# Norm rows loaded as broadcasts, and the order of work around the last two expert units, in a decoder layer on one core

## The chip, the cores and the metric

The kernel runs on one core of a Trainium2 chip. The core has five engines with an instruction queue each: TensorE (PE; its weight loads are listed as PEld) for matrix products and transposes, VectorE (DVE), ScalarE (ACT), GpSimd (POOL), and SyncE (SP), which here does nothing but ask for transfers. The engines meet only at semaphores. The metric is the device time of one execution in microseconds (us).

## The reference

One post-norm decoder layer is computed in float32 for one sequence of 512 tokens of width 1024. Two attention branches are mixed, projected and normalised; the part that matters here is the second half:

```python
x = layer_norm(DEEPNORM_ALPHA * x + gate1 * attn_out, ln1_g[l], ln1_b[l])
u2 = x * (1.0 + scale2) + shift2
moe = hierarchical_moe(u2.reshape(B * S, D), ...)   # (1)
x = layer_norm(DEEPNORM_ALPHA * x + gate2 * moe, ln2_g[l], ln2_b[l])

# (1) for every group of experts; combine is zero except for a token's two experts
h = silu(einsum('nd,edf->nef', t, w_g[sl])) * einsum('nd,edf->nef', t, w_u[sl])
h = h * combine[:, sl, None]
out = out + einsum('nef,efd->nd', h, w_d[sl])
```

There are 32 experts of width 256 in 4 groups. A token goes to the best group, and there to the best two of 8 experts.

## The kernel before

The first 430 us are projections, attention and the first norm. The normalised rows are written to DRAM twice: `xnd` holds them for the rows 0 to 255 already scaled by ln1's gain and shift and by the factor alpha, `xhd` without. Then come the experts.

**Units.** Tokens are sorted by expert into slots. Two experts (a pair, 64 rows each) or four (a quad, 32 rows each) make one unit with a row tile of 128. There are 12 units; the last two, unit 10 and unit 11, are quads. A unit is worked through in these steps: gate and up products (`gate_up`, L1352, 64 matmuls into one bank `pgu`), Silu on ScalarE and the product with up on VectorE (`act_h`, L1360 and L1361), the transpose of the result (`h_tr`, L1367, and `h_copy`, L1375), down products (`down`, L1382, two halves of 16 matmuls for a quad), evacuation times `gate2` (`y_evac`, L1392), and a scatter of the rows to the DRAM tensor `Ys` (`y_store`, L1398, on GpSimd). Larger tiles of a unit (`tiles`) are behind branches on the counted rows; here they aren't taken.

**Weights.** They rotate through 15 buffers (`ex_3506` and the like). `load_gran` (L940 for gate and up, L943 for down) is called for the second unit after the present one, right behind the present one's evacuation, and asks on SyncE. A request for an expert with no tokens moves nothing. SyncE's requests take eight semaphores in turn, so each waits until the transfer eight places before it is done.

**Order.** The engines TensorE, GpSimd and SyncE take their instructions in the order in which the code is written (`manual_schedule`). VectorE and ScalarE are ordered by a scheduler, except in the first and the last part, which is written out too.

**The last unit's result** isn't scattered. It stays on the chip, and its rows are added by a product with a selection matrix: `select_rows` (L1433 to L1437, GpSimd) builds for each of four token tiles which of the unit's rows belongs to which token, with which weight; `select_tr` (L1447 and L1448) turns this by eight transposes on TensorE and two copies on ScalarE. `diagonals` makes eight diagonal matrices of the tokens' weights on VectorE.

**Norm rows.** The gains and shifts of both norms have 1024 numbers each, and are wanted on all 128 partitions. `norm_rows` loads all four into 16 rows of a small tile early among the units, `scale_rows` multiplies ln1's by alpha with three small VectorE operations, and `broadcast` (L1460, L1461) spreads one row by products of a column of the identity with the small tile, which ScalarE copies out. ln2's two are spread behind `select_tr`, ahead of unit 10's down products; ln1's two between the two halves of the last unit's gate and up products. At an earlier place, in the middle of the kernel, ln1's two rows are loaded as broadcasts straight from DRAM instead, and scaled on ScalarE (L964 and L965); that place is the same in both kernels.

**Branch.** Ahead of the last unit stands `overflow()` (L1465 and L1466), a branch for experts with more tokens than their slot, which isn't taken here. All five engines pass it. Behind it SyncE asks for the rows of `xnd` and `xhd` (L1619, L1620).

**Tail.** For each of four row tiles of 128 tokens, TensorE adds up in two banks of 512 columns: the last unit's selected rows (`add_sel`, L1672), for the right half the residual (`add_x`, L1669) and the two rows gathered from `Ys` times the diagonals (`add_dg`, L1679). For the left half VectorE adds the residual (`base`, L1683) and the gathered rows (`add_y`, L1686). The moments, the norm and the output follow (L1690 to L1746). The gathered rows are asked for by SyncE at L1660, two requests of 0.52 MB for each row tile. GpSimd scales the residual of row tiles 2 and 3 with ln1's rows (`scaled`, L1646 and L1649).

## Time and profile before

| what | value |
| --- | --- |
| median of the runs shown | 787.19 us (786.98 to 790.57, 3 runs) |
| the profiled execution, its own time | 786.38 us |
| its span from the first to the last instruction | 784.70 us |
| mean granted clock of TensorE | 0.937 of full speed |
| busy: TensorE | 678.0 us, 86% of the span |
| busy: VectorE, ScalarE, GpSimd | 480.5, 252.5, 173.8 us |
| transfers | 184.13 MB, 235 GB/s in the mean |

The rows further down come from one profiled execution. Times are counted from the span's start. The execution's own time is 1.68 us longer than the span. The busy shares are means over stages with different limits. In timelines, neighbouring instructions of one form stand in one row with their count; in brackets is the engine's idle time ahead of the row and what the trace takes to have ended it. "PEq" or "POOLq" as releaser is the queue of an engine at a branch.

### The profile page before, as it was taken

To read this page: it belongs to the slowest core of one execution; us is meant where nothing else is said; L and a number is where in the kernel's file an instruction comes from. 1 tells how busy PE (TensorE), PEld (TensorE's weight loads), DVE (VectorE), ACT (ScalarE), POOL (GpSimd) and SP (SyncE) were. 2 spreads that over 40 slices of the span, in tenths; PEclk is the share of its full clock that TensorE was granted. 3 is DMA by queue.
4 is the path that set the end of the run, shared out by engine and by line. 5 is a ranking of instruction groups with operands and counts; after the bars stand their busy time and mean duration, and the time that the engine had idled before them with its cause. 6 is when DMAs were issued, how large, how long until landed. Compare 5 with 4: busy or idle time off the path is not lost. (4 is left out here: it accounts for less than half of the span.)

```text
span 784.7 us, 10759 instructions
## 1 busy us (share of the span) xinstructions
PE 678.0 (86%) x3361; PEld 426.8 (54%) x3361; DVE 480.5 (61%) x1070; ACT 252.5 (32%) x546; POOL 173.8 (22%) x240
## 2 busy tenths in 40 slices
PE   5999998989989998799999873977699699976983
PEld 4778766556757765566788662432363223333321
DVE  3353479877775558977595686774825606551158
ACT  2233344433333434444341453622101101122221
POOL 2007024122233313200000013111111101155155
PEclk9999999999999999999999895889899989996897
DMA  9959763365653011361369468796999989799652
GB/s 281 360 159 332 241 200 107 112 220 200 221 168 107 18 31 42 108 196 54 107 215 368 169 259 295 236 389 241 411 407 417 386 342 351 280 404 395 236 215 107
DMA packets 83230, 184.13 MB, mean 235 GB/s; under 512 B 15201, under 2 KB 48590, under 8 KB 77274
## 3 DMA queue, kind: packets, MB, share of 16 engines
q1 hardware_dynamic: 76608, 171.71, 60.9%
q0 software_dynamic: 6480, 11.53, 4.2%
q8 instruction: 37, 0.61, 0.3%
q14 instruction: 31, 0.25, 0.1%
q10 hardware_dynamic: 74, 0.03, 0.0%
HBM read 173.28 MB, written 28.33 MB: 257 GB/s over the span
## 5 line engine op out<-in xcount | busy, mean ns | idle before, releaser
L1352 PE MATMUL pgu<-ex,xT 128*64 128x512 f32 (+1 forms) x608 | 116.1, 619 | 9.9 <-DMA ex<-in_w_exp_up_dram 5.8
L330 PE MATMUL acc<-uh,whi 128*128 128x512 f32 x224 | 91.8, 410 | 1.1 <-ACT whi L320 1.1
L330 PE MATMUL acc<-uh,wlo 128*128 128x512 f32 x224 | 89.1, 398 | 2.4 <-DVE wlo L321 2.4
L1352 PEld LDWEIGHTS pgu<-ex,xT 128*64 128x64 f32 (+1 forms) x608 | 52.4, 130 | 69.4 <-issue 63.8
L330 PE MATMUL acc<-ul,whi 128*128 128x512 f32 x224 | 89.1, 398 | 0.0
L1382 PE MATMUL py<-ex,hT 128*64 128x512 f32 (+1 forms) x304 | 63.8, 673 | 10.8 <-DVE rtx L1392 4.4
L628 POOL TENSOR_TENSOR w<-be,sc 128x128 f32<-128x128 f32 (+3 forms) x32 | 41.8, 1314 | 119.8 <-DVE sc L626 60.6
L1360 ACT ACTIVATE sl<-pgu 128x256 f32<-128x256 f32 x33 | 11.5, 382 | 167.7 <-PE pgu L1352 122.9
L321 DVE TENSOR_TENSOR wlo<-raw,whi 128x1024 fp32r<-128x1024 f32 x27 | 38.9, 1448 | 21.4 <-ACT whi L320 17.8
L330 PEld LDWEIGHTS acc<-uh,wlo 128*128 128x128 f32 x224 | 42.6, 190 | 14.8 <-DVE wlo L321 3.5
L1398 POOL DMA_INDIRECT Ys<-w,msk_mla x11 | 10.9, 989 | 178.2 <-DVE w L1392 150.2
L330 PEld LDWEIGHTS acc<-uh,whi 128*128 128x128 f32 x224 | 42.8, 191 | 11.7 <-ACT whi L320 1.6
L330 PEld LDWEIGHTS acc<-ul,whi 128*128 128x128 f32 x224 | 42.9, 192 | 9.0 <-issue 0.8
L1361 DVE TENSOR_TENSOR sl<-pgu,sl 128x256 f32<-128x256 f32 x33 | 12.9, 418 | 52.0 <-ACT sl L1360 47.8
L1382 PEld LDWEIGHTS py<-ex,hT 128*64 128x64 f32 (+1 forms) x304 | 16.8, 134 | 51.1 <-issue 30.5
L449 DVE SCALAR_TENSOR_TENSOR macc<-ra,rtx,macc 128x1024 f32<-128x1024 f32 x28 | 41.5, 1523 | 3.6 <-DMA ra<-in_w_ada_dram 3.6
L626 DVE TENSOR_TENSOR_SCAN sc<-al 128x127 f32<-128x127 f32 (+3 forms) x32 | 28.7, 921 | 12.7 <-ACT al L622 12.7
L320 ACT CAST whi<-raw 128x1024 fp32r<-128x1024 f32 x27 | 28.1, 1050 | 24.9 <-PE acc L330 9.8
L1375 DVE COPY hT<-phT 128x256 f32<-128x256 f32 x33 | 13.1, 418 | 37.3 <-PEq L1408 21.8
L563 PE MATMUL px<-ident,w 128*128 128x128 f32 x160 | 26.7, 279 | 9.2 <-POOL w L628 5.0
L563 PEld LDWEIGHTS px<-ident,w 128*128 128x128 f32 x160 | 18.5, 142 | 17.5 <-issue 7.1
L895 PE MATMUL oh<-wo,mixh 128*128 128x512 f32 x64 | 23.9, 430 | 1.4 <-DVE wo L877 1.4
(494 smaller groups left out, 1387.1 us busy)
## 6 DMA issues: line engine op xcount, KB each, us to landing
ex<-in_w_exp_gate_dram SPq DMA_DIRECT2D x64, 512.0 KB
ex<-in_w_exp_up_dram SPq DMA_DIRECT2D x64, 512.0 KB
ex<-in_w_exp_down_dram SPq DMA_DIRECT2D x32, 1024.0 KB
ra<-in_w_ada_dram SPq DMA_DIRECT2D x16, 1024.0 KB
raw<-in_w_in_dram SPq DMA_DIRECT2D x12, 1024.0 KB
ada<-in_w_ada_dram SPq DMA_DIRECT2D x6, 1024.0 KB
rwo<-in_w_out_dram SPq DMA_DIRECT2D x6, 1024.0 KB
Ys<-dqh SPq DMA_DIRECT2D x8, 512.0 KB
```

The costliest lines, as they stand in the source:

```text
L320: ACT.copy(hi, w)
L321: DVE.tensor_tensor(lo, w, hi.bitcast(F32), ALU.subtract)
L330: PE.matmul(a, w_[:, k, :], part(u_, k), start=(k == 0 and n == 0), stop=(k == nk - 1 and n == 2))
L449: DVE.scalar_tensor_tensor(o, v, cact[:, k, 0:1], o, ALU.mult, ALU.add)
L563: PE.transpose(px[:, kt * P:(kt + 1) * P], w[:, kt * P:(kt + 1) * P], ident)
L626: DVE.tensor_tensor_scan(sc[:, 0:W - 1][:, ::-1], al[:, 1:W][:, ::-1], al[:, 1:W][:, ::-1], 1.0, ALU.mult, ALU.bypass)
L628: POOL.tensor_tensor(w[:, 0:W], be[:, 0:W], sc[:, 0:W], ALU.mult)
L895: PE.matmul(a, u_, w_[:, k % 4, :], start=first and n == 0, stop=last and n == 2)
L1352: PE.matmul(ps_t[rows, :], xT[u, t][:, k, rows], ew[e, k // 4][:, :, k % 4, :], start=(k == 0), stop=(k == KD - 1))
L1361: DVE.tensor_tensor(sl, ps_t[:, DE:2 * DE], sl, ALU.mult)
L1375: DVE.tensor_copy(hT[u, min(t, 1)][:, t // 2], phT[:, o:o + 256].rearrange("p (k n) -> p k n", k=2))
L1382: PE.matmul(pys[nh][rows, :], hT[u, min(t, 1)][:, t // 2, k, rows], ew[e, 2][:, k, nh * 512:(nh + 1) * 512], start=(k == 0), stop=(k == 1))
```

## The change

- The four broadcasts by products, the small tile, and the loads and operations that fill it go. In their place SyncE asks for four loads behind the branch, right after those of `xnd` and `xhd`, that write each of the four rows to all 128 partitions from DRAM. ln1's two are multiplied by alpha by one ScalarE operation ahead of GpSimd's scaling of row tile 2.
- `select_rows` is called before the work of units 8 and 9, not at its end.
- `select_tr` and `diagonals` stand behind the branch, ahead of the last unit's gate and up products, which run without a break between the halves.
- A Silu of a tile of one number stands behind the branch (`warm`), and the one of the square root takes another input.
- The products of the residual for row tiles 0 and 1 (`add_x`) are written first, to follow the last unit's transposes; the banks of the sums are dealt out differently, and the tail's loop has `add_x` only for row tiles 2 and 3.

```diff
--- before.py
+++ after.py
@@ -1364,7 +1364,8 @@
         o = 256 if t == 1 else 0
         h = hs[u, min(t, 1)][:, t // 2, :].rearrange("p (q k) -> p k q", k=2)
         for k in range(2):
-            PE.transpose(phT[:, o + k * P:o + (k + 1) * P], h[:, k, :], ident)
+            i = PE.transpose(phT[:, o + k * P:o + (k + 1) * P], h[:, k, :], ident)
+        return i.ins
 
     def h_copy(u, t):
         if t >= u.ntl:
@@ -1411,19 +1412,6 @@
 
     lng1, xv, *axr = (egran[i].rearrange("p (a d) -> p a d", a=2) for i in (6, 8, 7, 9))
     lng2 = [rtx[:, 0:D], None]
-
-    lr16 = rtx[0:16, 1024:1280]
-    acol = cp.tile([16, 1], F32, name="acol")
-
-    def norm_rows():
-        for i, v in enumerate((ln2_g, ln2_b, ln1_g, ln1_b)):
-            SP.dma_start(lr16[4 * i:4 * i + 4], v[0].rearrange("(c n) -> c n", c=4))
-
-    def scale_rows():
-        DVE.reduce_sum(acol, ident[0:16, 8:16], axis=AX.X)
-        DVE.tensor_scalar(acol, acol, ALPHA - 1.0, 1.0, ALU.mult, ALU.add)
-        DVE.tensor_scalar(lr16, lr16, acol, None, ALU.mult)
-
 
     selw = gate1.rearrange("p (a t n) -> p a t n", a=2, t=NT)
 
@@ -1451,14 +1439,6 @@
         for t in range(NT):
             for j in range(2):
                 DVE.tensor_scalar(dg[:, t, j, :], ident, w12[j][:, t:t + 1], None, ALU.mult)
-
-    def broadcast(v, dst):
-        for h in range(2):
-            pb = pt("z", 2, "pb")
-            for q in range(2):
-                r = 4 * v + 2 * h + q
-                PE.matmul(pb[:, q * 256:(q + 1) * 256], ident[0:16, r:r + 1].to_broadcast([16, P]), lr16, start=True, stop=True)
-            ACT.copy(dst[:, h * 512:(h + 1) * 512], pb)
 
 
     def overflow():
@@ -1561,6 +1541,8 @@
         for n, u in enumerate(units):
             more = n + 1 < len(units)
             un = units[n + 1] if more else None
+            if 2 + NOV // 2 <= n < 4 + NOV // 2:
+                select_rows(n - 2 - NOV // 2)
             pipe = n > 0 and more and u.nb == 2 and un.nb == 2
             if pipe:
                 ps0 = pt("fil", 2, "pgu0")
@@ -1576,18 +1558,12 @@
                 last = tc.manual_schedule(engines={mybir.EngineType.DVE, mybir.EngineType.Activation})
                 last.__enter__()
             if n > 0 and not pipe:
-                h_tr(u, 0)
+                htr_at = h_tr(u, 0)
                 h_copy(u, 0)
             xcopy(n + 2, 0)
             if n > 0:
                 xcopy(n + 1, 1)
                 xcopy(n + 1, 2)
-            if n == len(units) - 2:
-                select_tr()
-                lng2[1] = tmp("whi", [D], F32, "lng2")
-                broadcast(0, lng2[0])
-                broadcast(1, lng2[1])
-                diagonals()
             py0 = [pt("z", 2, f"py0_{n}") for n in range(2)]
             down(u, 0, py0, (0,))
             tiles(u, f, lambda t: h_tr(u, t))
@@ -1616,15 +1592,18 @@
                 order.close()
                 overflow()
                 order.enter_context(tc.manual_schedule(engines=MS))
+                ACT.activation(warm, warm, AF.Silu)
+                lng2[1] = tmp("whi", [D], F32, "lng2")
                 SP.dma_start(axr[0], xnd.rearrange("(t p) d -> p t d", p=P))
                 SP.dma_start(xv, xhd[256:512, :].rearrange("(t p) d -> p t d", p=P))
+                for v, o in ((ln1_g, lng1[:, 0]), (ln1_b, lng1[:, 1]), (ln2_g, lng2[0]), (ln2_b, lng2[1])):
+                    SP.dma_start(o, v[0].partition_broadcast(P))
             if more and not pipe:
                 ps0 = pt("fil", 2, "pgu0")
-                gate_up(un, 0, ps0, range(4))
                 if n == len(units) - 2:
-                    for v in range(2):
-                        broadcast(2 + v, lng1[:, v])
-                gate_up(un, 0, ps0, range(4, KD))
+                    select_tr()
+                    diagonals()
+                gate_up(un, 0, ps0)
                 act_h(un, 0, ps0)
                 if n == 0:
                     more_tiles(1)
@@ -1632,17 +1611,14 @@
                     y_store(u, (0, 1, 2))
             if n == 2 + NOV // 2:
                 DVE.tensor_copy(ovi, ov[0:1, :, 0:2])
-            if n == 1:
-                norm_rows()
-                scale_rows()
-            if 2 + NOV // 2 <= n < 4 + NOV // 2:
-                select_rows(n - 2 - NOV // 2)
 
 
         hc = [slice(h * 512, (h + 1) * 512) for h in range(2)]
         rs = [axr[t // 2][:, t % 2, :] for t in range(NT)]
 
         def scaled(e, t):
+            if t == 2:
+                ACT.activation(lng1, lng1, AF.Copy, scale=ALPHA)
             e.tensor_tensor(rs[t].rearrange("p (q k) -> p q k", k=KD), xv[:, t % 2, :].rearrange("p (k q) -> p q k", k=KD),
                             lng1[:, 0].rearrange("p (q k) -> p q k", k=KD), ALU.mult)
             for h in (1, 0):
@@ -1659,9 +1635,9 @@
             for j in range(2):
                 SP.dma_start(gt[:, j, :], Ys[j * S + t * P:j * S + (t + 1) * P, :])
             gts.append(gt)
-        ACT.activation(warm, dg[0:1, 0, 0, 0:1], AF.Sqrt, scale=0.0)
-        sums = {(t, h): pt(b, n, "sums") for h, bs in ((0, (("fil", 2), ("fil", 2), ("m", 1), ("t", 2))),
-                                                       (1, (("av", 1), ("z", 2), ("z", 2), ("t", 2)))) for t, (b, n) in enumerate(bs)}
+        ACT.activation(warm, yb[0][0:1, 0:1], AF.Sqrt, scale=0.0)
+        sums = {(t, h): pt(b, n, "sums") for h, bs in ((1, (("fil", 2), ("fil", 2), ("z", 2), ("t", 2))),
+                                                       (0, (("av", 1), ("z", 2), ("m", 1), ("t", 2)))) for t, (b, n) in enumerate(bs)}
         for t in (2, 3):
             scaled(POOL, t)
 
@@ -1706,10 +1682,12 @@
             o = rs[t][:, hc[h]]
             e.tensor_tensor(o, o, lng2[1][:, hc[h]], ALU.add)
 
-        add_x(0)
+        for t in range(2):
+            with tc.issue_after(htr_at):
+                add_x(t)
         for t in range(NT):
             add_sel(t, 0)
-            if t:
+            if t > 1:
                 add_x(t)
             add_sel(t, 1)
             add_sel1(t)
```

TensorE, around unit 10's down products, before: `phT` are the transposes of `h`, `pse` those of the selection rows, `pb` the broadcasts, and `py_0_7389` is the left half of the down products, with the four weights' buffers behind the arrow.

```order
L1408 UNCONDITIONAL_BRANCH x2
L1367 MATMUL phT<-ident,sl 128x128 x2
L1447 MATMUL pse<-ident,gate 128x128 x8
L1460 MATMUL pb<-rtx,ident 128x256 x8
L1382 MATMUL py_0_7389<-ex_3400,hT 32x512
L1382 MATMUL py_0_7389<-ex_3506,hT 32x512
L1382 MATMUL py_0_7389<-ex_3509,hT 32x512
L1382 MATMUL py_0_7389<-ex_3658,hT 32x512
```

In the changed kernel the same eight transposes stand behind the overflow branch, ahead of the last unit's gate and up products (`pgu_7520`):

```order
L1447 COMPARE_AND_BRANCH
L1447 UNCONDITIONAL_BRANCH
L1446 UNCONDITIONAL_BRANCH x2
L1435 MATMUL pse<-ident,gate 128x128 x8
L1352 MATMUL pgu_7520<-ex_3813,xT_7018 32x512
L1352 MATMUL pgu_7520<-ex_3853,xT_7018 32x512
L1352 MATMUL pgu_7520<-ex_3855,xT_7018 32x512
L1352 MATMUL pgu_7520<-ex_3857,xT_7018 32x512
```

So the down products follow the transposes of `h` at once, and the transposes and the broadcasts that stood between have moved behind the branch, or are gone.

ScalarE, from the branch to the tail's first square root, before: `pb` are the broadcasts of ln1's rows, `sl` the last unit's Silu, `mv` the moments.

```order
L1466 UNCONDITIONAL_BRANCH x2
L1461 ACT_TABLE_LOAD
L1461 COPY ex_3506<-pb 128x512 x4
L1360 ACT_TABLE_LOAD
L1360 ACTIVATE sl<-pgu_7560 128x256
L1408 UNCONDITIONAL_BRANCH
L1360 ACTIVATE sl<-pgu_4090 128x256
L1408 UNCONDITIONAL_BRANCH x4
L1692 ACT_TABLE_LOAD
L1692 ACTIVATE mv<-mv,epsr 128x1
```

The same place in the changed kernel, where `sely` is the turned selection matrix and `ex_3506` the buffer of ln1's rows:

```order
L1446 UNCONDITIONAL_BRANCH x2
L1436 COPY sely<-pse 128x512 x2
L1360 ACTIVATE sl<-pgu_7520 128x256
L1409 UNCONDITIONAL_BRANCH
L1360 ACTIVATE sl<-pgu_4089 128x256
L1409 UNCONDITIONAL_BRANCH
L1638 ACT_TABLE_LOAD
L1638 ACTIVATE warm<-w 1x1
L1409 UNCONDITIONAL_BRANCH
L1621 ACTIVATE ex_3506<-ex_3506 128x2048
```

No table load stands ahead of the Silu there, and the one for the square root stands right behind it.

SyncE, behind the branch, before: `gt_7711` and so on are the buffers of the gathered rows.

```order
L1619 DMA ex_3509<-xnd 128x2x1024
L1620 DMA ex_3658<-xhd 128x2x1024
L1408 UNCONDITIONAL_BRANCH
L1660 DMA gt_7711<-Ys 128x1024 x2
L1660 DMA gt_7714<-Ys 128x1024 x2
```

And in the changed kernel:

```order
L1597 DMA ex_3509<-xnd 128x2x1024
L1598 DMA ex_3658<-xhd 128x2x1024
L1600 DMA ex_3506<-in_ln_g_dram 128x1024
L1600 DMA ex_3506<-in_ln_b_dram 128x1024
L1600 DMA rtx<-in_ln_g_dram 128x1024
L1409 UNCONDITIONAL_BRANCH
L1600 DMA lng_7513<-in_ln_b_dram 128x1024
L1636 DMA gt_7676<-Ys 128x1024
```

The four broadcast loads stand between the loads of rows and the requests for the gathered rows.

## Rows read from the trace of the kernel before

**Rows 1.** Chain that ended last, first and last step: start us, us, engine, output, line

```profile
765.17 0.69 DVE sums L1683
...
780.50 0.75 DVE ex L1745
```

**Rows 2.** Timeline of VectorE: start us, us, instruction, count [idle before, releaser]

```profile
732.88 0.68 DVE L1392 TENSOR_TENSOR sc<-py,gate 128x512 f32<-128x512 f32 x1
...
765.17 0.69 DVE L1683 TENSOR_TENSOR sums<-ex,sums 128x512 f32<-128x512 f32 x1 [1.07 <-PEq L1408]
```

**Rows 3.** Timeline of TensorE from 711 to 760, columns as in rows 2

```profile
711.26 0.71 PE L1447 MATMUL pse<-ident,gate 128*128 128x128 f32 x5
...
718.43 7.19 PE L1460 MATMUL pb<-rtx,ident 16*128 16x256 f32 x16
725.55 3.64 PE L1382 MATMUL py<-ex,hT 128*32 128x512 f32 x16
729.37 2.15 PE L1382 MATMUL py<-ex,hT 128*32 128x512 f32 x16 [0.18 <-PEq L1408]
732.78 4.05 PE L1352 MATMUL pgu<-ex,xT 128*32 128x512 f32 x32 [1.26 <-DMA ex<-in_w_exp_down_dram]
736.76 4.09 PE L1460 MATMUL pb<-rtx,ident 16*128 16x256 f32 x16
740.78 4.98 PE L1352 MATMUL pgu<-ex,xT 128*32 128x512 f32 x32
748.07 0.50 PE L1367 MATMUL phT<-ident,sl 128*128 128x128 f32 x2 [2.31 <-DVE sl L1361]
...
749.46 1.92 PE L1382 MATMUL py<-ex,hT 128*32 128x512 f32 x16
...
755.76 1.96 PE L1679 MATMUL sums<-gt,gate 128*128 128x512 f32 x4
...
758.41 1.02 PE L1669 MATMUL sums<-ex,ident 128*128 128x512 f32 x2
```

**Rows 4.** Timeline of GpSimd: scatter, first and last selection operation, first scaling

```profile
693.48 0.97 POOL L1398 DMA_INDIRECT Ys<-w,msk_mla  x1 [10.77 <-DVE w L1392]
...
697.09 0.55 POOL L1433 TENSOR_SCALAR onesf<-iot 128x128 f32<-128x128 f32 x1
...
717.51 0.45 POOL L1437 TENSOR_TENSOR gate<-gate,rk 128x128 f32<-128x128 f32 x1
...
746.04 2.86 POOL L1646 TENSOR_TENSOR ex<-ex,ex 128x1024 f32<-128x1024 f32 x1 [10.47 <-PEq L1408]
```

**Rows 5.** Busy us of each engine (instructions), granted clock, DMA share and GB/s by stretch

```profile
431.00:432.00 1.00, 1.00 (x6) 0.84 (x5) 1.00 (x2) 0.00 (x0) 0.00 (x0) 1.00 1.08 266
718.00:726.00 8.00, 7.98 (x21) 5.54 (x25) 0.29 (x1) 4.07 (x7) 0.00 (x0) 0.50 0.99 369
731.00:732.00 1.00, 0.52 (x8) 0.00 (x0) 0.32 (x1) 0.00 (x0) 0.00 (x0) 1.00 0.68 279
735.00:736.00 1.00, 1.00 (x15) 0.74 (x9) 0.00 (x0) 0.00 (x0) 0.57 (x1) 1.00 0.53 160
736.00:738.00 2.00, 2.00 (x13) 1.08 (x7) 0.00 (x0) 0.07 (x1) 0.00 (x0) 1.00 1.03 408
```

**Rows 6.** Timeline of SyncE's queue, last requests; columns as in rows 2

```profile
717.36 0.07 SPq L940 DMA_DIRECT2D ex<-in_w_exp_up_dram  x1
...
724.94 6.82 SPq L943 DMA_DIRECT2D ex<-in_w_exp_down_dram  x4
733.68 0.40 SPq L1619 DMA_DIRECT2D ex<-xnd  x1
...
745.92 4.60 SPq L1660 DMA_DIRECT2D gt<-Ys  x8
```

**Rows 7.** Timeline of ScalarE, at the middle and in the last part

```profile
433.77 1.91 ACT L965 ACTIVATE lng<-lng 128x2048 f32<-128x2048 f32 x1 [6.22 <-DMA lng<-in_ln_b_dram]
...
745.88 1.28 ACT L1360 ACT_TABLE_LOAD   x1 [4.41 <-PE pgu L1352]
```

## The prediction

> **What bounds the kernel now.** I read the chain that ended last first. It names VectorE alone, from 765 us to the end at 781.25, and shares out 2% of the span: it breaks off at the first wait that it can't follow [rows 1]. So the question is what released VectorE there. VectorE's timeline answers: its add for row tile 2 at 765.17 had sat idle for 1.07 us until TensorE's branch had passed [rows 2]. TensorE's timeline therefore comes next, and it has to be read backwards from there [rows 3]. In the tail it adds up the four row tiles without a pause, 4.7 us each: the gathered rows' products of the first begin at 755.76 and those of the third release VectorE at 765.17. They follow the down products of the last unit (749.46), which follow its gate and up products, which end at 745.76. Before these stand the down products of unit 10 (725.55), and before them 16 records of broadcast products that begin at 718.43, and transposes that began at 711.26. The transposes need GpSimd's selection rows, of which the last is written at 717.51 [rows 4]. That stretch is what the change takes apart. A further 16 broadcast records stand inside the last unit's gate and up products, at 736.76.
>
> The second thing to see is the transfers. The weights stream at some 400 GB/s until 731.7: in the microsecond from 731 there are 279 GB/s, 0.68 of the 408 of a full one [rows 5]. SyncE asks for the next transfer only at 733.68, and for the gathered rows at 745.92 [rows 6]. So TensorE's path can be shortened only until the stream is the limit, and what the change adds to the stream counts.
>
> The profiled execution took 786.38 us, 1.68 more than its span of 784.70; the median of the runs shown is 787.19, 0.81 above it. I sum against the profiled execution and add 0.81 at the end. Times below that stand for the changed kernel are on the old trace's scale.
>
> **The change part by part.** *Selection rows earlier.* On GpSimd the first selection moves ahead of unit 8's scatters, the second ahead of unit 9's. Both took 20.9 us from 697.09 to the end at 717.96 with two scatters of some 1.3 us each between them, so 9.1 us each [rows 4]. GpSimd had sat idle for 10.77 us ahead of unit 8's scatters at 693.48 [rows 4], which hides the first. If VectorE's overflow items hold it back, it is the scatters that come late, by up to 9.1 us. That would cost unit 10's activation at most some 2 us, and behind that the weights wait anyway (next part). I take nothing, and 2 us as the other end, also covered.
>
> *Transposes and broadcasts out of the way of unit 10's down products.* What stood ahead of them from 711.26 to 725.55 is gone: 14.3 us. But they can't start at 711.9. A SyncE request waits for the transfer eight places before it; the one at 717.36 moves nothing itself (0.07 us, its expert has no tokens) and waited for the fourth of unit 10's down loads [rows 6]. The fourth product in TensorE's order needs that load. So the start is 717.4, and I let them take what they took: 3.64 + 0.18 + 2.15, to 723.3 [rows 3]. At the rate of the last unit's (1.92 each) it would be 721.4; I take the slow one because TensorE will have idled from 712.
>
> *The transposes' new place.* They now wait for VectorE to pass the overflow branch. Its last evacuation ended at 733.56, 2.04 after the last down product [rows 2, 3]; TensorE needed 1.26 from its last product to its first behind the branch, and I give VectorE the same. So 723.3 + 2.04 + 1.26 = 726.6. Five of the transposes took 0.71 us at full rate [rows 3], so eight take 1.1, or 2.3 at half rate: 728.3 in the middle. On ScalarE the two copies that follow are beside TensorE's work, as are VectorE's eight diagonals.
>
> *Gate and up of the last unit without the broadcasts between.* The halves took 3.98 (732.78 to 736.76) and 4.98, the second after a slow start; 4.09 of broadcasts between them go [rows 3]. With 4.05 for each and half a microsecond for the slow start they end at 736.9. Their weights are there: the last to land are the two down loads of 2.1 MB, 5.1 us of stream before 731.7.
>
> *The table request.* In the order on ScalarE it brings no load with it, and the load ahead of the Silu at 745.88, 1.28 us, is gone [rows 7]. From the last product to the transposes of h there were 2.31 us; 1.03 are left: 737.9.
>
> *Four broadcast loads, 0.52 MB each, and the scaling.* Removed for them: four requests and three small VectorE operations in the middle of the kernel, where neither engine is waited for. SyncE asks for them right behind the two loads of rows, ahead of the gathered rows. All weights must have landed first (731.7); the request that used to wait for unit 10's last product, and left at 731.76 (the four from 724.94 took 6.82) [rows 6], is no longer late. I put the first request at 733.0, between 732.3 and the old 733.7. Data began 1.9 us after it (the microsecond from 735 had 160 GB/s), so at 734.9. The first row load, 1.05 MB at 408 GB/s, is there at 737.5, just ahead of the transposes that its product follows. Then: second row load and four broadcasts to 734.9 + 4.19/0.408 = 745.2, and the first pair of gathered rows to 747.8. With 0.5 us (an estimate, 0 to 1) until the waiting engine moves: 748.3.
>
> TensorE meanwhile: last down products at 737.9 + 1.39 = 739.3 instead of 749.46, the gathered rows' products 6.30 later as before (749.46 to 755.76) plus 0.9 for the second residual product, which now stands ahead: 746.5. So the gathered rows end last, at 748.3; the second half of the 1.96 us block follows: 749.3 instead of 757.72, 8.4 us earlier. The second tile then lacks its residual product (1.02 us with its drain, 0.9 without [rows 3]), so from the second tile's end on all is 9.3 us earlier, VectorE's add of 765.17 too.
>
> The scaling took 1.91 us at its other place, waiting for its own two broadcast loads [rows 7]. Here they land at 743.1 (3.15 MB and 0.5 us), behind the warm-up that waits for the last unit's first evacuation (741.9 or so): done at 745.0. GpSimd's two tiles need 2.86 and as much again each [rows 4], so they are ready at 750.7 and 756.4; they are wanted at 755.9 and 760.6. That leaves over 4 us.
>
> **Sum:** 786.38 - 9.3 + 0.81 = 777.9; I say 778.
>
> What is unknown is the rate of the broadcast loads. At the other place the microsecond that I can give to them had 266 GB/s, the lowest of that stretch [rows 5]: 7.9 us instead of 5.1, and 780.7. At no cost of their own at all TensorE's path would be last, at 746.5, and the time 777.2. I take 408, since the row loads ran at it.
>
> The Trainium skill speaks against such loads: "DMA: Bandwidth & Descriptors", section "Bandwidth", asks for at least 1 MiB per transfer to get 75% of the peak and gives 341 GB/s at 1 MB. By 341 for all six loads the pair would come 2.0 us later and the time would be 779.9; the 408 GB/s of row loads of 1.05 MB that ran two at a time [rows 5] speak for the higher rate.
>
> **Rivals.** *The last unit still waits for the stream.* The trace ends TensorE's wait at 732.78 with a down load [rows 3]. If that holds, gate and up start there and end at 740.8, the gathered products come at 750.4 and end at 752.4: 5.3 + 0.9 us gained, 781.0. Against it: in the order those products wait for gate and up loads only, and 1.26 us is what the branch may take. 12 in 100.
>
> *TensorE at half clock after each wait.* From 718 to 726 it was granted 0.50, the 1.2 GHz level, though busy, after it had stood waiting for GpSimd; 16 records of down products took 3.64 us then, and 1.92 at the other level [rows 3, 5]. The changed kernel waits at three places (712, 723 and around 738). If gate and up lose 2.0 us more than I gave, the second half of unit 10's down products 1.5, the transposes 0.6, the last down products 1.7 and the residual product 0.9, TensorE's path ends 6.7 us later, at 753.2, and the time is 783 to 784. It begins to count after the first 0.8 us. 9 in 100, since 2.31 us of waiting at 745.8 left the next products at 1.92.
>
> The Trainium skill's "TensorE: Matmul & The Clock Gate", Part 1, has 1.2 GHz as the state after idling, which sides with this rival; the rows at 749.46 show that not every wait brings it.
>
> *The broadcasts at half the rate.* 10.3 us, gathered rows 5.1 later, 783.0. 9 in 100.
>
> *Slower: the broadcasts hold up the gathered rows.* Every partition reads the same 4 KB row. If that runs at a quarter of the rate, they take 20.6 us, the gathered rows land at 763.7, and the time is 6 us over the old, 794. It decides from 14.4 us, or 145 GB/s, on. For it: no row shows such loads by themselves. Against it: no microsecond around the other pair fell below 266. 8 in 100.
>
> **Chances and range.** The forecast has 62 in 100. What a measurement can tell from no change is about 0.5%, 3.9 us. Faster by more: the forecast, the first rival and parts of the next two, 85. Within: 7. Slower: 8. The range goes from 776.0, where the loads cost less and the clock holds, to 783.3, which takes in the half rate and most of the clock's case.
>
> **What would show it.** Unit 10's down products at about 717, the eight transposes at 726 to 729, one unbroken run of gate and up ending near 737, no table load ahead of the Silu, row loads asked for near 733, and TensorE waiting for gathered rows once, near 747. Wrong would be: gate and up beginning after 732, a wait for the first residual product of over 2 us, or gathered rows after 752. The prediction fails as a whole if the broadcast loads take over 10 us.

## The result and the profile after

The changed kernel took 776.79 us in the median of four runs (775.6 to 779.26), the kernel before 787.43 beside it (786.98 to 790.57): a ratio of 0.9874, with a 95% interval of 0.984 to 0.9908. 778 had been forecast, with 776.0 to 783.3 as range. Later series have it a little less fast: 779.2 against 786.85 (0.9911, 0.9876 to 0.9945) and 780.13 against 785.64 (0.9931, 0.9903 to 0.9959). So it is faster by 5.5 to 10.6 us in the medians of three series, and the time hit the forecast. The steps that were to give it did so only in part.

The profiled execution took 776.91 us, its span is 775.2. Executions differ ahead of the part that is changed, so everything below is also counted from one **mark**: the transposes of unit 10's `h`, the last work of TensorE ahead of the places at which the change alters its order. They stand at 710.92 in the profile before and at 707.99 here:

```profile
710.92 0.51 PE L1367 MATMUL phT<-ident,sl 128*128 128x128 f32 x2 [0.93 <-DVE sl L1361]
```

```profile
707.99 0.50 PE L1367 MATMUL phT<-ident,sl 128*128 128x128 f32 x2 [0.93 <-DVE sl L1361]
```

From the mark to the end of the span it was 73.8 us before and is 67.2 now: 6.6 of the 9.5 us that the span is shorter. The other 2.9 were there before the mark, 1.9 of them at the same transposes of the first unit, ahead of everything that the change touches (TensorE, first before, then after):

```profile
504.27 0.40 PE L1367 MATMUL phT<-ident,sl 128*128 128x128 f32 x2
```

```profile
502.35 0.40 PE L1367 MATMUL phT<-ident,sl 128*128 128x128 f32 x2
```

TensorE's timeline after the change, from unit 10's down products to the first tile's gathered rows (answers to [rows 3]):

```profile
709.01 1.05 PE L1383 MATMUL py<-ex,hT 128*32 128x512 f32 x4 [0.52 <-DVE hT L1376]
712.01 1.91 PE L1383 MATMUL py<-ex,hT 128*32 128x512 f32 x2 [1.95 <-DMA ex<-in_w_exp_down_dram]
714.57 5.30 PE L1383 MATMUL py<-ex,hT 128*32 128x512 f32 x26 [0.65 <-DMA ex<-in_w_exp_down_dram]
722.11 1.06 PE L1435 MATMUL pse<-ident,gate 128*128 128x128 f32 x8 [2.24 <-DVEq L1446]
723.10 7.07 PE L1352 MATMUL pgu<-ex,xT 128*32 128x512 f32 x64
731.19 0.50 PE L1367 MATMUL phT<-ident,sl 128*128 128x128 f32 x2 [1.01 <-DVE sl L1361]
736.92 2.05 PE L1645 MATMUL sums<-ex,ident 128*128 128x512 f32 x2 [5.23 <-DMA ex<-xnd]
738.90 3.02 PE L1383 MATMUL py<-ex,hT 128*32 128x512 f32 x16
...
747.16 1.95 PE L1655 MATMUL sums<-gt,gate 128*128 128x512 f32 x4
```

The down products begin at once, wait for two weight loads, and run on from 714.57, 6.6 after the mark; the prediction had 6.5. The eight transposes come at 722.11, the 64 products of gate and up run in one piece of 7.07 us, and the transposes of the last unit's `h` follow 1.01 after VectorE. All this is what the change was to do. VectorE's last evacuation ahead of the branch:

```profile
721.22 0.68 DVE L1393 TENSOR_TENSOR sc<-py,gate 128x512 f32<-128x512 f32 x1
```

TensorE's transposes follow its end (721.90) by 0.21. Ahead of the first residual product comes a wait that the prediction had named as the sign of being wrong: 5.23 us for the first row load. What follows it is slow: the two records of that product take 2.05 us, against 1.11 at the other place ahead of the down products and 1.10 here for the second tile's; the first 16 down records take 3.02 instead of 1.92.

SyncE's requests, and what the transfers and the clock did meanwhile (answers to [rows 6] and [rows 5]):

```profile
722.44 2.88 SPq L943 DMA_DIRECT2D ex<-in_w_exp_down_dram  x4
732.00 0.39 SPq L1597 DMA_DIRECT2D ex<-xnd  x1
```

```profile
729.00:730.00 1.00, 1.00 (x12) 0.13 (x4) 0.00 (x0) 0.00 (x0) 0.00 (x0) 1.00 0.54 189
732.00:734.00 2.00, 0.00 (x0) 0.00 (x0) 0.15 (x1) 0.25 (x1) 0.00 (x0) 1.00 0.20 55
734.00:737.00 3.00, 0.08 (x1) 0.11 (x1) 0.00 (x0) 0.00 (x0) 0.00 (x0) 0.55 1.02 416
737.00:741.00 4.00, 4.00 (x14) 0.99 (x18) 0.00 (x0) 0.00 (x0) 0.00 (x0) 0.50 1.03 420
...
742.00:743.00 1.00, 0.90 (x10) 0.38 (x14) 0.92 (x2) 0.00 (x0) 0.00 (x0) 1.00 0.78 209
```

The row load is asked for at 732.00. It was to be 733.0 on the old scale, 22.1 after the mark; it is 24.0. The weights' transfers end at about 729.5 (the microsecond from 729 has a share of 0.54), and data move again from about 733.7 on. SyncE had asked for its last weights by 725.3; in the profile before it did so only at 731.76 [rows 6], and asked for the first rows 2 us later. The third column from the right is the granted clock: 0.55 in the mean of three microseconds of waiting, and 0.50, the level of 1.2 GHz, in the four that follow. The transfers run at 416 and 420 GB/s in stretches that hold the row loads and the first of the broadcasts, and fall to 209 in the microsecond from 742. In the mean of the 12 us from 734 on, which hold all six loads, it is 391 GB/s; at the same place of the two later profiles of the change, 375 and 379.

ScalarE's Silu without a load ahead of it, and GpSimd's first scaling (answers to [rows 7] and [rows 4]):

```profile
730.29 0.66 ACT L1360 ACTIVATE sl<-pgu 128x256 f32<-128x256 f32 x2 [6.39 <-issue]
730.97 1.28 ACT L1638 ACT_TABLE_LOAD   x1
```

```profile
703.20 0.46 POOL L1425 TENSOR_TENSOR gate<-gate,rk 128x128 f32<-128x128 f32 x1
...
745.36 2.85 POOL L1622 TENSOR_TENSOR ex<-ex,ex 128x1024 f32<-128x1024 f32 x1 [21.55 <-PE sums L1645]
```

The selection rows are done at 703.66, 18.5 us ahead of the transposes that want them. GpSimd's first scaling starts when ScalarE has multiplied ln1's rows (743.36 to 745.27), not at TensorE's product that the row names.

### The profile page after: what moved, and what is told of

Same layout as the page of the kernel before. It is cut to its first block, busy times and chain, and to the rows that moved or that the text cites. A ratio compares the mean times of both kernels' runs of the same rounds, so it can differ in the third digit from the quotient of the medians.

```text
span 775.2 us, 10683 instructions
## 1 busy us (share of the span) xinstructions
PE 666.9 (86%) x3329; PEld 418.0 (54%) x3329; DVE 480.4 (62%) x1067; ACT 245.9 (32%) x537; POOL 173.8 (22%) x240
## 5 line engine op out<-in xcount | busy, mean ns | idle before, releaser
L1352 PE MATMUL pgu<-ex,xT 128*64 128x512 f32 (+1 forms) x608 | 113.5, 609 | 8.6 <-DMA ex<-in_w_exp_up_dram 5.8
L1383 PE MATMUL py<-ex,hT 128*64 128x512 f32 (+1 forms) x304 | 66.8, 676 | 14.0 <-DVE hT L1376 7.0
L321 DVE TENSOR_TENSOR wlo<-raw,whi 128x1024 fp32r<-128x1024 f32 x27 | 38.8, 1447 | 21.5 <-ACT whi L320 21.4
L1383 PEld LDWEIGHTS py<-ex,hT 128*64 128x64 f32 (+1 forms) x304 | 17.2, 135 | 57.3 <-issue 30.1
L449 DVE SCALAR_TENSOR_TENSOR macc<-ra,rtx,macc 128x1024 f32<-128x1024 f32 x28 | 41.6, 1524 | 3.7 <-DMA ra<-in_w_ada_dram 3.7
L1393 DVE TENSOR_TENSOR sc<-py,gate 128x512 f32<-128x512 f32 x24 | 16.3, 685 | 11.6 <-PE py L1383 7.2
```

Source lines behind the costliest of these rows:

```text
L321: DVE.tensor_tensor(lo, w, hi.bitcast(F32), ALU.subtract)
L449: DVE.scalar_tensor_tensor(o, v, cact[:, k, 0:1], o, ALU.mult, ALU.add)
L1352: PE.matmul(ps_t[rows, :], xT[u, t][:, k, rows], ew[e, k // 4][:, :, k % 4, :], start=(k == 0), stop=(k == KD - 1))
L1383: PE.matmul(pys[nh][rows, :], hT[u, min(t, 1)][:, t // 2, k, rows], ew[e, 2][:, k, nh * 512:(nh + 1) * 512], start=(k == 0), stop=(k == 1))
L1393: DVE.tensor_tensor(y[:, cols_], pys[nh], gate2[:, cols_], ALU.mult)
```

## The experiments

All profiles, one execution each, from the mark (us), and the times beside runs of the kernel before on the same chip. "Request" is SyncE's for the first row load, "residual" the first residual product, "gathered" the gathered rows' products of the first and of the last tile.

| kernel | mark | to the end | request | residual | gathered | median (ratio, 95%) |
| --- | --- | --- | --- | --- | --- | --- |
| before | 710.92 | 73.8 | 22.8 | 37.5 | 44.8, 58.9 | 787.19 |
| before, again | 709.17 | 73.9 | 23.3 | 37.7 | 45.0, 59.1 | 784.86 (one run) |
| after | 707.99 | 67.2 | 24.0 | 28.9 | 39.2, 52.4 | 776.79, 0.9874 (0.984 to 0.9908) |
| after, again | 712.02 | 69.1 | 24.1 | 30.1 | 41.0, 54.2 | 779.2, 0.9911 (0.9876 to 0.9945) |
| after, third | 707.07 | 69.6 | 24.2 | 30.7 | 41.6, 54.8 | 780.13, 0.9931 (0.9903 to 0.9959) |
| selection early alone | 708.99 | 66.7 | 23.3 | 30.5 | 37.8, 51.9 | 779.79, 0.9927 (0.9892 to 0.9963) |
| norm rows by products | 707.25 | 72.4 | 24.2 | 36.2 | 44.3, 57.5 | 782.39, 0.9965 (0.9926 to 1.0004) |
| selection late again | 713.32 | 68.4 | 25.0 | 30.0 | 39.8, 53.5 | 780.51, 0.9927 (0.9897 to 0.9958) |
| transposes ahead again | 710.69 | 68.0 | 24.9 | 29.9 | 39.7, 53.1 | 779.64, 0.9923 (0.9894 to 0.9951) |
| residual behind down | 707.67 | 69.2 | 23.5 | 31.8 | 39.3, 54.3 | 779.65, 0.9937 (0.9898 to 0.9975) |
| loads in order of need | 706.48 | 65.5 | 24.0 | 28.5 | 37.3, 50.8 | 777.95, 0.9908 (0.9875 to 0.9941) |
| residuals where needed | 708.77 | 65.3 | 23.7 | 31.2 | 34.2, 50.5 | 777.15, 0.99 (0.9869 to 0.9931) |
| no Silu request | 706.80 | 67.4 | 24.3 | 29.3 | 39.3, 52.5 | 778.69, 0.9923 (0.9893 to 0.9952) |
| both ways mixed | 705.66 | 63.7 | 24.0 | 29.3 | 32.2, 49.2 | 775.65, 0.9895 (0.9852 to 0.9937) |

Most intervals overlap; the stretches from the mark tell more than the times. But three profiles of the one changed kernel differ by 2.4 us there, so a difference of 1 or 2 us between two kernels is not shown by one profile of each.

**The kernel before, again.** Nothing is edited.

> The unchanged kernel before, profiled once more, to see how much its stages differ from one execution to the next. The first profile of the changed kernel comes to the transposes of unit 10's h at 707.99 us, 2.93 earlier than the kernel before (710.92), though nothing that the change does lies ahead of it. Theory A (chance of one execution, above all the granted clock around 440 us): this run comes there somewhere between 707 and 712, and not at the same place as the first profile within 0.3 us. Theory B (the removed small loads or another order upstream give 2.9 us in every execution): within 0.5 us of 710.9.

TensorE's timeline of this run, the mark:

```profile
709.17 0.51 PE L1367 MATMUL phT<-ident,sl 128*128 128x128 f32 x2 [0.93 <-DVE sl L1361]
```

The mark is 1.75 us earlier than in the first profile, the stretch behind it the same within 0.2. That speaks for theory A. The clock around 440 us, which theory A named, does differ: from 437 to 443 us the first profile of before had it at 0.50, that of after at 1.00.

```profile
437.00:443.00 6.00, 5.69 (x19) 5.04 (x20) 2.39 (x5) 2.40 (x4) 0.00 (x0) 0.50 0.41 128
```

```profile
437.00:443.00 6.00, 4.44 (x29) 3.93 (x28) 3.88 (x8) 3.72 (x7) 0.00 (x0) 1.00 0.21 53
```

But it doesn't explain where the mark falls. The run without the Silu request had 0.50 there too and an early mark (706.80), the run with the late selection 1.00 and the latest of all (713.32). In all 14 profiles it is 205.1 to 206.8 us from the first unit's transposes of `h` to the mark, while those transposes themselves stand anywhere between 500.1 and 507.3. So the spread arises ahead of the units; from what, is not shown.

**The changed kernel, again.** Nothing is edited.

> The changed kernel once more. From the transposes of unit 10's h to the end of the span the first profile took 67.2 us, against 73.8 before, so that only 6.6 of the 9.5 us less come from the part that the change touches, where my sum had 9.3. Theory A (the rest is chance upstream): the stretch behind takes 67.2 within 0.5 us again, and the stretch ahead differs from 708.0 by up to 3 us. Theory B (a steady gain upstream): 708.0 within 0.5 us. Time 775 to 779 by both.

TensorE's timeline of this run, the mark, the wait and what follows it:

```profile
712.02 0.51 PE L1367 MATMUL phT<-ident,sl 128*128 128x128 f32 x2 [0.93 <-DVE sl L1361]
...
742.14 2.05 PE L1645 MATMUL sums<-ex,ident 128*128 128x512 f32 x2 [3.60 <-issue]
744.12 3.64 PE L1383 MATMUL py<-ex,hT 128*32 128x512 f32 x16
```

The mark is 4.03 us later than in the first profile of the same kernel, so the 2.9 us upstream were not a gain that each execution has. The other half of what theory A said was wrong too: the stretch isn't steady, but 69.1. The residual comes 6.05 us after the request instead of 4.92, and the whole first half of the down products ran at the lower level, 3.64 us.

**Early selection alone.** In the kernel before, the two lines of `select_rows` stand at the head of the loop:

```diff
         un = units[n + 1] if more else None
+        if 2 + NOV // 2 <= n < 4 + NOV // 2:
+            select_rows(n - 2 - NOV // 2)
         pipe = n > 0 and more and u.nb == 2 and un.nb == 2
...
-            if 2 + NOV // 2 <= n < 4 + NOV // 2:
-                select_rows(n - 2 - NOV // 2)
```

> One part of the change alone: the kernel before, with the selection rows built ahead of the work of units 8 and 9; transposes, broadcasts by products, the branch and the tail stay as they were. Theory R (the row loads of SyncE decide behind the branch, TensorE has some 5 us to spare in the changed kernel): the transposes no longer wait for GpSimd, the 16 broadcast records end near 720, unit 10's down products near 726, the last unit's gate and up with the broadcasts between near 739, so that TensorE gains some 6.5 us: 780 to 782. Theory S (my sum: only with the broadcasts out of TensorE's way are the 9 us to be had): the same mechanism gives at most the 6 us of waiting for GpSimd, 781 to 783, but the broadcasts keep 8 us on the path. Rival (the weights take back what the transposes gain): 785 to 787.

TensorE's timeline of this run:

```profile
709.33 1.04 PE L1447 MATMUL pse<-ident,gate 128*128 128x128 f32 x8
710.66 1.99 PE L1460 MATMUL pb<-rtx,ident 16*128 16x256 f32 x8 [0.29 <-ACT sely L1448]
713.13 2.67 PE L1460 MATMUL pb<-rtx,ident 16*128 16x256 f32 x8 [0.48 <-ACT rtx L1461]
715.73 3.64 PE L1382 MATMUL py<-ex,hT 128*32 128x512 f32 x16
...
739.12 0.51 PE L1367 MATMUL phT<-ident,sl 128*128 128x128 f32 x2 [2.31 <-DVE sl L1361]
...
746.81 1.96 PE L1679 MATMUL sums<-gt,gate 128*128 128x512 f32 x4
```

The transposes no longer wait, and the broadcasts behind them take 5.1 us from first to last instead of 7.19, at a granted clock of 1.00 until 714, where the kernel before had 0.50 [rows 5]. They fill the time in which the down products would wait for their weights. The stretch is 66.7 us, 7.1 shorter than before, and no longer than that of the whole change; the ratio of the times (0.9927) makes it 5.7 us. Both theories had 6 to 6.5. TensorE comes to the last unit's transposes 30.1 after the mark, 4 to 7 later than in the three profiles of the change (23.2, 26.0 and 26.4), but finds the rows there and gathers its rows 1.4 earlier than the best of them.

**Norm rows by products.** The broadcasts by products come back into the changed kernel, without the loads:

```diff
                 if n == len(units) - 2:
                     select_tr()
+                    broadcast(0, lng2[0])
+                    broadcast(1, lng2[1])
                     diagonals()
-                gate_up(un, 0, ps0)
+                gate_up(un, 0, ps0, range(4))
+                if n == len(units) - 2:
+                    for v in range(2):
+                        broadcast(2 + v, lng1[:, v])
+                gate_up(un, 0, ps0, range(4, KD))
```

> The changed kernel with one part undone: the norm rows are spread by products again (ln2's behind the selection's transposes, ln1's between the halves of the last unit's gate and up), no broadcast loads, nothing scaled on ScalarE; all the rest as changed. 8.2 us of broadcasts come back onto TensorE between the branch and the last unit's transposes, and 2.1 MB leave the stream ahead of the gathered rows. Theory R (TensorE waits 5.2 us for the first row load there, so that the products fill a wait): the last unit's transposes come near 739.5 instead of 731.2, the first residual product no longer waits, the down products start at the same time within 1.5 us, and the clock no longer falls to half there: 775 to 779, the same as the changed kernel. Theory S (my sum, TensorE's path 1.8 us ahead of the gathered rows): the 8.2 us lengthen the path by some 6.4, 783 to 785.

TensorE's timeline of this run, and one stretch of it:

```profile
722.50 6.56 PE L1462 MATMUL pb<-rtx,ident 16*128 16x256 f32 x16 [0.30 <-issue]
728.99 5.81 PE L1352 MATMUL pgu<-ex,xT 128*32 128x512 f32 x32
```

```profile
723.00:733.00 10.00, 10.00 (x35) 5.12 (x38) 0.15 (x1) 2.35 (x4) 0.00 (x0) 0.51 0.60 221
```

Theory R was wrong here, and S was near. The broadcasts took 6.56 and 3.79 us, not 8.2 in all, and pulled the gate and up products with them to the lower clock. The wait for the row load was filled, and 3 to 5 us were added: gathered rows at 44.3 after the mark, against 39.2 to 41.6 with the change. So behind the branch the loads are worth that much against products. Where half of the products stand ahead of unit 10's down products, as in the run of the early selection alone, nothing of it is seen.

**Selection late again.** In the changed kernel the two lines of `select_rows` go back to the loop's end.

```diff
-            if 2 + NOV // 2 <= n < 4 + NOV // 2:
-                select_rows(n - 2 - NOV // 2)
             pipe = n > 0 and more and u.nb == 2 and un.nb == 2
...
             if n == 2 + NOV // 2:
                 DVE.tensor_copy(ovi, ov[0:1, :, 0:2])
+            if 2 + NOV // 2 <= n < 4 + NOV // 2:
+                select_rows(n - 2 - NOV // 2)
```

> The changed kernel with the selection rows built where the kernel before built them, behind unit 8's and 9's scatters; all the rest as changed. In the run of the early selection alone the stretch from unit 10's transposes of h to the end took 66.7 us, as little as in the whole change (67.2 and 69.1). Theory R (the two are different ways out of one wait: either the rows are early or the transposes are late): the transposes stand behind the branch near 722, GpSimd is done near 715, so nothing waits: stretch 66.5 to 69.5, time as the changed kernel, 775 to 780. Rival (the early rows are what the change lives on): transposes wait again, stretch 71 or more, 783 and up.

GpSimd's last selection operation and TensorE's transposes and first residual product in this run:

```profile
720.23 0.46 POOL L1425 TENSOR_TENSOR gate<-gate,rk 128x128 f32<-128x128 f32 x1
```

```profile
727.54 1.07 PE L1435 MATMUL pse<-ident,gate 128*128 128x128 f32 x8 [2.24 <-DVEq L1446]
...
743.34 2.04 PE L1645 MATMUL sums<-ex,ident 128*128 128x512 f32 x2 [6.21 <-DMA ex<-xnd]
```

GpSimd is done 6.9 us ahead of the transposes, and the stretch is 68.4, as theory R had it. With the run of the early selection alone this shows one wait, that of the transposes for GpSimd, and two ways out of it, of which either is enough.

**Transposes ahead again.** `select_tr()` and `diagonals()` go back ahead of unit 10's down products in the changed kernel.

```diff
+            if n == len(units) - 2:
+                select_tr()
+                diagonals()
             py0 = [pt("z", 2, f"py0_{n}") for n in range(2)]
...
-                if n == len(units) - 2:
-                    select_tr()
-                    diagonals()
                 gate_up(un, 0, ps0)
```

> The changed kernel with selection transposes and diagonals back ahead of unit 10's down products; the rows are early, so they don't wait. Theory R (unit 10's down products wait for their weights until 714.6 anyway, and TensorE waits 5 us for the row load behind): 1.1 us of transposes lie in the wait for weights, the last unit's gate and up start 1 us earlier, and the row load takes it all back: stretch 66.5 to 69.5, time the same as the changed kernel, 775 to 780. Theory S (my prediction: the new place is worth something): 1 to 2 us longer.

TensorE's timeline of this run, the transposes and the first residual product:

```profile
711.03 1.04 PE L1435 MATMUL pse<-ident,gate 128*128 128x128 f32 x8
...
740.55 2.05 PE L1645 MATMUL sums<-ex,ident 128*128 128x512 f32 x2 [7.24 <-DMA ex<-xnd]
```

TensorE is 1.1 us earlier at the last unit's transposes and waits 7.24 us for the row load: the stretch is 68.0, within those of the change. That fits theory R; with their spread, the 1 us at the lower end of theory S can't be ruled out.

**No Silu request.** The line `ACT.activation(warm, warm, AF.Silu)` is taken out of the changed kernel.

> The changed kernel without the Silu of one number behind the branch. In the order of its instructions no table load stands ahead of the last unit's Silu either, so that the missing load would be the work of the copies that went, and not of the request. Both theories of the table load (request or not) then give the same time, since TensorE waits 3.6 to 7.2 us for the first row load right behind: stretch 66.5 to 69.5, 775 to 780. If a load of 1.28 us does appear, the wait takes it up, with the same time.

ScalarE's timeline of this run:

```profile
729.00 0.66 ACT L1360 ACTIVATE sl<-pgu 128x256 f32<-128x256 f32 x2 [6.39 <-issue]
729.67 1.28 ACT L1637 ACT_TABLE_LOAD   x1
```

No load stands ahead of the Silu, so in the changed kernel the request does nothing. A load stands there in the kernel before, and in the early selection alone with its 2.31 us ahead of the transposes; in the run of the norm rows by products (1.01 us) there is none, though the copies of broadcasts are back. The kernel before shows what else differs: its request for the square root ran ahead of the branch, between the selection's copies and those of the broadcasts, and brought a table load with it.

```profile
719.14 1.28 ACT L1662 ACT_TABLE_LOAD   x1
```

So another table than Silu's was loaded between unit 10's Silu and the last unit's. With its other input, that request comes behind the last Silu (its load stands at 730.97 in the changed kernel). No run changes this input alone, so that it is the cause is argued from the order and not shown.

**Residual behind down.** The first two residual products of the changed kernel follow the last down products.

```diff
-            down(u, 0, py0, (1,))
+            down_at = down(u, 0, py0, (1,))
...
-            with tc.issue_after(htr_at):
+            with tc.issue_after(down_at):
                 add_x(t)
```

> The changed kernel with the first residual product behind the last unit's down products instead of ahead of them, so that TensorE doesn't stand waiting for the first row load (5.2 and 3.6 us in the two profiles) ahead of work that needs no rows. Theory S (the gathered rows land behind rows and broadcasts near 746.5 on the first profile's scale): the wait comes back ahead of the gathered rows' products, which start at most 0.7 us earlier: stretch 66 to 68.5, 775 to 779. Theory R (they are there earlier, and the order on TensorE alone holds the tail up): gathered rows' products 4 to 5 us earlier, stretch 62 to 64, 771 to 774.

TensorE's timeline of this run:

```profile
735.13 1.92 PE L1383 MATMUL py<-ex,hT 128*32 128x512 f32 x16 [0.56 <-issue]
...
747.01 3.35 PE L1656 MATMUL sums<-gt,gate 128*128 128x512 f32 x4 [3.87 <-DMA gt<-Ys]
```

The wait came back as theory S had it: 3.87 us, now for the gathered rows, 39.3 after the mark, where the change has 39.2 to 41.6. Now those products ran slow (3.35 instead of 1.96). So two things end close together in the changed kernel, TensorE's order and the landing of the gathered rows, and undoing one shows the other.

**Loads in order of need.** The edit of the run before stays. Besides, the six requests behind the branch go, and SyncE asks tile by tile in the tail.

```diff
+        for t in range(NT):
+            if t < 2:
+                SP.dma_start(axr[0][:, t, :], xnd[t * P:(t + 1) * P, :])
+            if t == 1:
+                rows((ln1_g, lng1[:, 0]), (ln1_b, lng1[:, 1]))
+                SP.dma_start(xv, xhd[256:512, :].rearrange("(t p) d -> p t d", p=P))
+            if t == 2:
+                rows((ln2_g, lng2[0]), (ln2_b, lng2[1]))
             gt = gran(etags[10 + t], [2, D], F32, f"gt{t}")
```

> The one before it, and SyncE's requests behind the branch in the order in which the tail needs them: the first row tile of the residual alone (0.5 MB), the first pair of gathered rows, the second residual tile, ln1's two rows, the residual of tiles 2 and 3, the second pair, ln2's rows, the other pairs. Both theories have the first pair land some 3.8 us after the stream restarts instead of 12.8; TensorE's path is then last, with the gathered rows' products 6 to 7 us earlier than in the changed kernel, and GpSimd's scaling of tile 2 comes ready just when it is wanted: stretch 60 to 63, 769 to 773. If the later requests or GpSimd's scaling hold up tiles 2 and 3, 2 to 4 us of it are given back there: 772 to 776.

TensorE's timeline of this run:

```profile
739.10 1.71 PE L1653 MATMUL sums<-ex,ident 128*128 128x512 f32 x2 [3.03 <-DMA ex<-xnd]
...
743.76 1.96 PE L1663 MATMUL sums<-gt,gate 128*128 128x512 f32 x4
```

It gave 65.5, and 60 to 63 had been expected by both theories (769 to 773 us; the median is 777.95). What both had overlooked: the second residual product still stood ahead of the first tile's sums, and waited 3.03 us for its load.

**Residuals where needed.** On top of that, the second residual product goes to its tile, and the loads of ln1's rows and of tile 2 come ahead of the second residual load (only the edit of the products is shown).

```diff
-        for t in range(2):
-            with tc.issue_after(down_at):
-                add_x(t)
+        with tc.issue_after(down_at):
+            add_x(0)
         for t in range(NT):
             add_sel(t, 0)
-            if t > 1:
+            if t:
                 add_x(t)
```

> The run with the loads in order of need gained 1.2 us at most on the best stretch before it (65.5 against 66.7), because the second residual product still stood ahead of the first tile's sums: it waited 3.0 us for its load, and the next seven products ran at half clock, 1.7 us more. Here only the first residual product stands ahead; the second goes to its tile's place. The loads of ln1's rows and of the residual of tile 2, split from that of tile 3, come ahead of the second residual load, so that GpSimd's scaling starts near 5 us earlier. Theory (the order of TensorE's work against the landing of its loads is what is left): gathered rows' products of the first tile 4 to 5 us earlier than in that run, the last tile's about 3.5 us earlier, held by the last pairs' landing: stretch 61 to 63, 769 to 773. Rival (the stream of 8.4 MB behind the branch is what the tail waits for, in whatever order): last pair near 753 on that run's scale, stretch 64.5 to 66, 773 to 777.

TensorE's timeline of this run:

```profile
742.95 1.95 PE L1670 MATMUL sums<-gt,gate 128*128 128x512 f32 x4 [0.15 <-PEq L1410]
...
746.45 1.13 PE L1660 MATMUL sums<-ex,ident 128*128 128x512 f32 x2 [0.69 <-DMA ex<-xnd]
...
754.13 1.12 PE L1670 MATMUL sums<-gt,gate 128*128 128x512 f32 x2 [1.01 <-DMA gt<-Ys]
```

The first tile comes 3.1 us earlier than in the run before it, but the second waits for its residual and the third for its gathered rows (1.01 us): 65.3. The rival holds: in another order the stream is waited for at another tile, and the stretch is the same.

**Both ways mixed.** ln2's rows by products, ahead of unit 10's down products with the transposes; ln1's by loads; the rest as in the run with the residuals where needed (the load of the small tile and the products' code are left out here).

```diff
+            if n == len(units) - 2:
+                select_tr()
+                lng2[1] = tmp("whi", [D], F32, "lng2")
+                broadcast(0, lng2[0])
+                broadcast(1, lng2[1])
+                diagonals()
             py0 = [pt("z", 2, f"py0_{n}") for n in range(2)]
...
-                rows((ln2_g, lng2[0]), (ln2_b, lng2[1]))
```

> The run with the residuals where needed took 65.3 us from unit 10's transposes of h to the end; its sums waited for the third pair of gathered rows and the second residual load, so that the stream of 8.4 MB behind the branch held the tail. Here the stream loses 1.05 MB: ln2's rows are spread by products as in the kernel before, behind selection transposes ahead of unit 10's down products, whose weights are waited for there anyway; ln1's rows stay loads. Theory (the stream behind the branch is the tail's bound in the changed kernel): the third pair lands 2.5 us earlier, no wait is left at the third and fourth tile, stretch 62.5 to 64, 770 to 774. Rival (TensorE and VectorE behind the last unit set the tail, the wait was chance): stretch 65 to 66.5, 775 to 778; and if unit 10's down products are pushed out by more than the wait they fill, longer still.

TensorE's timeline of this run:

```profile
737.90 1.95 PE L1688 MATMUL sums<-gt,gate 128*128 128x512 f32 x4 [0.15 <-PEq L1410]
...
743.36 1.13 PE L1678 MATMUL sums<-ex,ident 128*128 128x512 f32 x2 [2.65 <-DMA ex<-xnd]
```

1.05 MB less in the stream, and no tile waits for gathered rows: 63.7, within what the stream's theory said, though the second residual load is still waited for (2.65). It is the shortest stretch of all, and the lowest median of the later series, but at 775.65 over the 770 to 774 of that theory; and 1.6 us less than in the run before it is within what three profiles of one kernel differ by. Its interval overlaps that of the changed kernel run beside it:

**The changed kernel beside it.** Nothing is edited.

> The changed kernel beside the run with both ways mixed, on the same chip and against the same runs of the kernel before. By all theories as twice before: 775 to 780, stretch 67 to 69.5, with a wait of 3.5 to 7 us for the first row load ahead of the first residual product, and the products behind it at the clock's lower level.

TensorE's timeline of this run:

```profile
737.78 2.05 PE L1645 MATMUL sums<-ex,ident 128*128 128x512 f32 x2 [3.80 <-issue]
739.76 3.64 PE L1383 MATMUL py<-ex,hT 128*32 128x512 f32 x16
```

The wait was 3.80 us, the stretch 69.6 and the median 780.13, both a little over what was expected.

## Why the prediction came out, point by point

Numbers are of the first profile of the change, where no other is named.

- **Unit 10's down products.** Right. They begin their last run 6.6 us after the mark (6.5 forecast) and end at 11.9 (12.4; 13.0 and 13.4 in the later two). The fourth weight load was what they waited for.
- **The transposes' new place.** Right in kind, 1.5 us too late in size: VectorE's last evacuation ended at 721.90, and TensorE began at 722.11, where 1.26 had been given to the crossing.
- **Gate and up in one piece.** They end 22.2 after the mark and not 26.0. The slow start that I had added came in the later two (7.90 and 8.21 us instead of 7.07; end at 25.0 and 25.4), not in this one.
- **The table load.** Its 1.28 us went, and 1.01 are left as forecast; the reason given, the request, wasn't needed for it, as its removal shows. The traces point to the square root's request, which no longer runs ahead of the branch.
- **SyncE's request.** This is the step that failed: "I put the first request at 733.0, between 732.3 and the old 733.7". On the mark's scale that is 22.1, and no kernel had it before 22.8; the changed one has 24.0, 24.1 and 24.2. The weights' transfers end 21.5 after the mark (at 729.5) and not 20.8, and SyncE asks 2.5 us after them, not 1.3. I had taken the late request for weights at 731.76 for a part of the old 2.0 us; in the changed kernel SyncE had made it by 725.3, and the 2.0 didn't shrink. So the row load, which was to be there "at 737.5, just ahead of the transposes that its product follows", became a load that TensorE waits for: TensorE was earlier than forecast, the load later.
- **The clock.** The rival of the half clock had 9 in 100 and was expected at three places. Much of it came. In all three profiles of the change it came at the first half of unit 10's down products, which the sum had slow anyway, and at the place where TensorE waits for the row load; at the start of gate and up it came in the later two. The row load's place cost 2.0 us in the first (2.05 and 3.02 against 1.11 and 1.92) and 2.7 in the others, and the sum had nothing for it. The Trainium skill's "TensorE: Matmul & The Clock Gate", Part 1, has the lower level as the state after idling. The granted clock of 0.50 behind 5.23 us of waiting agrees with it; the waits of 2.31 us before and 2.65 in the last mixture brought no slow products.
- **The broadcast loads.** Right within 4 to 8%: with the rows they ran at 391 GB/s in the mean, 375 and 379 in the later two, against the 408 taken, and neither the half nor the quarter rate came true. The Trainium skill's "DMA: Bandwidth & Descriptors", section "Bandwidth", gives 341 GB/s at 1 MB, measured with loads that GpSimd asks for; these, of 0.5 and 1 MB, asked for by SyncE with several in flight, ran faster than that.
- **The gathered rows as the binding landing.** Nearly. They were to land 37.4 after the mark; where TensorE stood waiting for them, with the residual behind down, its products began at 39.3. 1.4 us of the difference are the later request of that run (23.5), 0.5 the way from the request to the products (15.8, with 15.3 forecast).
- **The second residual product.** Its 0.9 us came back as forecast: 28.94 us from the first tile's gathered rows to the end before, 28.04 after.
- **Two slips without weight.** VectorE's add at 765.17 was released by the branch ahead of the third tile's gathered products (765.12), not by the products; and the quarter rate's sum gives 793, not 794.

**The sum.** Over three profiles of the change and two of before the stretch behind the mark is shorter by 5.2 us (68.6 against 73.9), not by 9.3. TensorE's forecast chain had the gathered rows' products at 35.6 after the mark; they came at 40.6 in the mean. 2.6 us of the difference lie in the later first residual product (29.9 instead of 27.3, 0.34 behind the forecast transposes of `h`), 2.4 between it and the gathered rows, most of it the clock. That the median of the first four runs still met the forecast is in part luck: the one of them that was profiled was 2.9 us early at the mark. The later medians of 779 and 780, of 10 and 12 runs, are the better measure. They are 7.7 and 5.5 us under the kernel before, where the forecast had 9.2. The likeliest case of the prediction was thus too good by 1.5 to 3.7 us in time and 4 in mechanism.

**What the gain is.** The wait of TensorE's transposes for GpSimd's selection rows, and with it the slow products behind the wait, some 7 us in all, is what the change removes. That is shown, by the early selection alone. Of the rest of the change, taken together, no run shows a gain beyond it. The broadcast loads take the 7.19 and 4.09 us of products [rows 3] off TensorE, but this time turns into waiting for SyncE's loads, to which they add 2.1 MB. That the stream decides there is supported by three runs (the wait that returned for the gathered rows, the two orders with one stretch, the mixture that is shorter with fewer bytes), but not shown. What stays open is why the first residual product came 6.05 and 6.47 us after its request in two of the three profiles of the change and 4.92 in the first; the trace names no releaser there. From the request to the product, 1.34 MB moved in the first, 1.49 and 1.96 in the others, of which the load itself is 1.05; so in the last of them, at least, the loads asked for behind it had moved a good part of their bytes by then.

## What to carry to other kernels

Before an engine's work is thinned out, look at what it will meet: here TensorE came to the last unit's transposes 11 to 14 us earlier and met a transfer that is asked for only when the weights have landed and a branch is passed. A product that waits for a load should not stand ahead of work that doesn't, and loads should be asked for in the order in which the tail wants them; here the first of these alone gained nothing (69.2), the two together 2 to 4 us. And where the stretch ahead of a change differs by several us from one execution to the next, count from a mark just ahead of the change.

## What the runs showed of the hardware

- TensorE came to the mark between 705.66 and 713.32 us in 14 profiles, and one and the same kernel between 707.07 and 712.02. Most of the spread was there at the first unit (500.1 to 507.3). The stretch from 437 to 443 us ran at a granted clock of 0.50 in one execution and at 1.00 in another, but the late marks aren't those with the low clock.
- SyncE needed 2.0 us (before) and 2.5 (after) from the end of the weights' transfers to the next request behind the branch, and data moved 1.7 us after that (after): some 4 us in which hardly anything is transferred, under 20 GB/s from 730 to 733.
- Loads of one 4 KB row to all partitions ran nearly as fast as loads of different rows: 375 to 391 GB/s over 12 us that hold both, against 407 from 736 to 740 in the kernel before, which hold rows alone.
